# Query tiles of a hybrid decoder step taken from the last to the first

## Chip, cores and metric

The kernel runs on one core of a Trainium2 chip. The metric is the time of one execution in device microseconds. Before the change the median of three runs is 656.16 us (655.71 to 656.98).

## What is computed

One inference step of a one-layer decoder for a prompt of 1024 tokens and 8 samples of one new token each, model width 1024, all in float32. Cut to what matters:

```python
h = rmsnorm(x); q, ckv, skv, wkv, gate_logits, za, u, zp = split(h @ w_in)
# (A) 8 query heads, 2 key heads, head size 64; per head and query block of 128
k_c, v_c = compress_blocks(ckv)                       # 63 compressed blocks of the prompt
o_c = softmax(q k_c, causal) v_c
o_s = softmax(q skv_k, causal, top 16 blocks of 64) skv_v   # 16 blocks: all of the prompt
o_w = softmax(q wkv_k, causal, last 512) wkv_v
o_attn = g0 * o_c + g1 * o_s + g2 * o_w               # g = sigmoid(gate_logits)
# (B) pooling over trailing windows of 2, 4, 8, 16 tokens
o_pool = ((window_mean(u) - u) @ w_pool) * pool_scale
mix = concat(o_attn * silu(za), o_pool * silu(zp))
y = rmsnorm(x + mix @ w_out)
```

The new keys, values and pooling states are outputs too.

## The kernel before

Every product is made of high and low parts of its factors, so it costs three products on TensorE (two where one operand holds both parts). The work runs in stages: norm, transposes and token-major projections of x; compressed keys and values; queries, which go out to scratch memory; the eight samples ("decode"); the pooling group with its gate; and, from 292.6 us on, attention over the prompt. Only this last stage is touched by the change.

**Units.** Attention runs over `UNITS` (line 686): for each query tile i of 128 tokens, i from 0 to 7, four pairs of heads j. Tile i sees i+1 selected blocks of 128 keys, the last five at most as window blocks, and 64 compressed keys. So tile 0 has 2 blocks a unit and tile 7 has 13.

**stage1** (line 702) makes the scores S of a unit (line 736; groups of at most 512 columns, through three PSUM banks), masks them and takes their maxima on VectorE (line 699), exponentiates on ScalarE (line 750) and scales by sum and gate on GpSimd (line 756), which gives the tiles Ps (compressed and selected) and Pw (window). **stage2** (line 829) transposes the result block by block (lines 845, 853), splits it into high and low part on ScalarE and VectorE (lines 847 to 859: pc, ph, pl), multiplies by the values (lines 864 to 871) into bank O, and at the end adds the two halves of O (lines 875 to 883) and multiplies by the gate, if that is there already. stage1 of the next unit runs inside stage2 of the present one.

**The filler** (`filler`, line 1039) is a generator of steps of three products on TensorE that stand between those of attention. First `za_fill` (line 916): the gate path, 12 chunks (a quarter of the gate's columns by a chunk of tokens, in the order of `ZORD`) of 8 steps each, over tokens 0 to 383, 384 to 767 and 768 to 1031 (`CHUNKS`); each chunk ends in `gate` (a tanh on ScalarE, line 902, and products on VectorE and GpSimd, lines 910 and 912). Once a chunk of x has been used by all four quarters, `load_wo` (line 936) puts rows of the output weights in its place, those that `WROWS` lists, and splits them (lines 947 and 948). Then `out_half` (line 1022): the output product of a tile, by halves of 512 columns, eight steps each; rows 4 to 7 of the weights' row blocks (the pooling part) first, then rows 0 to 3 (attention's part). `split_m` (line 959) splits the mixed output on ScalarE and GpSimd, `out_add` and `out_end` add x, norm and store. Tile 0 and the samples (tile 8) come first, then tiles 1 to 6, each only after its attention is done (`done`); of tile 7 the pooling part is made ahead, and its attention part closes the kernel (line 1134 on). All filling products share one PSUM bank, pj.

**What sets the order.** The program is planned by a scheduler that estimates times; attention has priority, filling steps get in where it would wait, and `paced_fill` (line 1081) gives out steps at a rate per unit: 0.8 times (blocks + 2) in the gate path, 0.5 times (blocks + 2) in the output products, 12 at the start. Each engine then works through its own list strictly in order. Query tiles (`load_q`) are loaded on SP's queue four units ahead.

Of the kernel before, what the change touches and what calls it, by code (L numbers as in the profile page):

```python
# [20 lines left out]
D = 1024  # L21
NEG = -1.0e9
# pacing of the filling products: steps per block of attention (gate path, output), blocks added per unit,
# steps at the start, lag in products
NZ, NO, C0, OW, PLAG = 0.8, 0.5, 2, 12, 100
ZORD = ([(0, 0), (0, 1), (0, 2), (1, 0), (1, 1), (1, 2)]
        + [(pt, c) for c in range(3) for pt in (2, 3)])
# the rows of the output weights, by half of their columns, that take the place of each chunk of x
WROWS = [[(0, k) for k in (4, 5, 6, 7, 0, 1)], [(0, 2), (0, 3)] + [(1, k) for k in (4, 5, 6, 7)],
         [(1, k) for k in range(4)]]  # L30
C_Q, C_C, C_S, C_W, C_G, C_ZA, C_U, C_ZP = 0, 512, 768, 1024, 1280, 1304, 1816, 2328
# [10 lines left out]
def hybrid_step_kernel(ctx, tc, xp, xs, ccmp, cslc, cwin, spool, ptab, norm_g, w_in, cmp_pe, cmp_w1,  # L42
# [33 lines left out]

    # DRAM scratch
    q_d = dram.tile([2, 512, T], F32, name="q_d")
# [3 lines left out]

    # constants
    ident = pers.tile([128, 128], F32, name="ident")
# [7 lines left out]
    def ptr_rms(pool, ssq, n, name):  # L92
        """(ssq / D + eps) ** -0.5 for a [n, 1] column."""
        st = pool.tile([128, 2], F32, name=name, tag="rms", bufs=4)
        nc.gpsimd.tensor_scalar(st[:n, 0:1], ssq, 1.0 / D, 1e-6, op0=OP.mult, op1=OP.add)
        nc.gpsimd.tensor_tensor(st[:n, 1:2], st[:n, 0:1], mhalf[:n], op=OP.pow)
        return st[:n, 1:2]

    # persistent data
    KT = pers.tile([128, 2, KLEN], F32R, name="KT")  # L100
# [64 lines left out]
    def spread_g(h):  # L165
        """The norm's weights from the first partition to all."""
        cs = slice(h * 512, h * 512 + 512)
        p = ps_any()
        nc.tensor.matmul(p, ones, gb[0:1, cs], start=True, stop=True)
        if h:  # L170
            nc.scalar.activation(gb[:, cs], p, AF.Copy)
        else:
            nc.vector.tensor_copy(gb[:, cs], p)

    # masks
    nc.gpsimd.memset(mslc, 0.0)
# [10 lines left out]

    # normalised x, transposed, as high and low parts
    rss = {}
# [35 lines left out]

    # token-major projections: compressed, selected and window keys and values, gate logits
    def tok_unit(hi, lo, cn, t, mid=None):
# [112 lines left out]
    nc.gpsimd.dma_start(g_d[:, :], gates[:NB, 8, :])  # L340
    # a token before the end of the first compressed block has no compressed branch
    vgate = pers.tile([128, 24], F32, name="vgate")
# [27 lines left out]
    def silu2(out, src):  # L370
        """2 * silu(src)"""
        nc.scalar.activation(out, src, AF.Tanh, scale=0.5)
        nc.vector.scalar_tensor_tensor(out, out, 1.0, src, op0=OP.add, op1=OP.mult)

    # page indices: row of 2 tokens each
    pti = keep.tile([128, NB], I32, name="pti")
# [10 lines left out]

    # compressed keys and values, prompt and samples
    ces = ExitStack()
# [98 lines left out]

    # queries
    for pt in range(4):  # L490
# [18 lines left out]
    def decode():  # L509
        """One new token per sample."""  # L510
        dp = des.enter_context(tc.tile_pool(name="dp", bufs=1, reuse_waits="tile"))
        # queries, one column per head and sample; qx: high parts, then low parts, per sample
        qs = dp.tile([128, NB, 8], F32, name="qs")
# [6 lines left out]
        def diag(ap):  # L520
            """The columns of each sample's own heads in [b, 2, 64] columns: [p, b, h]."""
            return bass.AP(tensor=ap.tensor, offset=ap.offset, ap=[ap.ap[0], [136, NB], [1, 8]])
# [59 lines left out]
        for br in range(2):  # L582
# [6 lines left out]
            for b in range(0, NB, 2):  # L589
# [8 lines left out]
                for bb in range(2):  # L598
# [7 lines left out]
                    for par in range(2):  # L606
                        nc.tensor.transpose(p[:, (bb * 2 + par) * 128:(bb * 2 + par + 1) * 128],
                                            f[:, par * 256:par * 256 + 128], ident)
                    # high and low parts of the values
                    v = dp.tile([128, 2, 2, 128], F32R, name="vx", bufs=8)  # L610
# [72 lines left out]

    # pooling group
    at = ctx.enter_context(tc.tile_pool(name="at", bufs=2, reuse_waits="tile"))
    UNITS = [(i, j) for i in range(8) for j in range(4)]
    q_tiles = {}
# [14 lines left out]
    def stage1(i, pr_):  # L702
        """Scores and softmax of a pair of heads for 128 queries; yields between matmul groups."""
        kv = pr_ // 2
# [6 lines left out]
        sm = at.tile([128, 2, 4, 3], F32, name="sm", bufs=3)  # L711
        # the first tile of a head: compressed 0:64, selected 64:64+n; the second: window 0:wn
        c_m = mc[:, 56 - 8 * i:120 - 8 * i]
# [47 lines left out]
    for g in range(4):  # L761
# [31 lines left out]
        if g == 2:  # L793
            load_q(0, 0)
            load_q(0, 1)
        if g == 3:
# [9 lines left out]
        for c in range(3):  # L806
# [7 lines left out]
            else:  # L814
                # the last on the engine that stores them
                nc.scalar.activation(bb[:, cs], p[:, :n], AF.Copy, scale=psc[:, g:g + 1])
# [5 lines left out]

    # attention over the prompt; the gate path, the new tokens and the output projection fill in
    zap = ctx.enter_context(tc.tile_pool(name="zap", bufs=1, reuse_waits="tile"))
# [4 lines left out]
    def stage2(i, pr_):  # L829
        """Transposes, products with the values and their sum; a list of steps."""  # L830
        kv = pr_ // 2
# [63 lines left out]

    # tiles of za that hold one factor of the gated output: the gate or the attention's output
    half_done = set()
# [38 lines left out]
    def load_wo(c):  # L936
        """Output weights in the place of x's chunk c, which is no longer needed."""
        rows = WROWS[c]
# [20 lines left out]
    def split_m(i, part):  # L959
        """High and low parts of four of the eight row blocks of the mixed output."""  # L960
        op = O_["p"]
# [77 lines left out]
    def filler():  # L1039
        yield from za_fill()  # L1040
        open_out()
        first = 0
        st = {}, {}
        for half in range(2):
            yield from out_half(first, half, st[0])
            yield from out_half(8, half, st[1])
        for i in range(1, 7):
            while done.get(i, 99) > now[0]:
                yield None
            st = {}  # L1050
            for half in range(2):
                yield from out_half(i, half, st)
        # the last tile: the pooling part ahead of its attention
        tail["r"] = load_r(7)
        m = parts(7, 1)
        tail["p"] = ps_j(), ps_s("pj2")
# [19 lines left out]
    def after(a, b):  # L1076
        """Keeps a behind b in their engine's order."""
        tc.add_manual_dep(a, b.name, mybir.DependencyInfo(
            mybir.DependencyClass.NoSync, mybir.DependencyReason.DATA), reason="order")

    def paced_fill(k):
        """Steps of the filler, none ahead of the attention's products emitted so far."""
        ins = nc.cur_bb.bb.instructions
# [49 lines left out]
    now[0] = 999  # L1133
    run(fill, 1000)
    L = 7
    op = O_["p"]
# [68 lines left out]
```

## Time and profile before

| | |
|---|---|
| Median of the runs | 656.16 us |
| Span of the profiled execution | 654.4 us |
| TensorE busy (PE) | 627.6 us, 96% |
| Weight loads busy (PEld) | 581.6 us, 89% |
| VectorE busy (DVE) | 426.0 us, 65% |
| ScalarE busy (ACT) | 361.0 us, 55% |
| GpSimd busy (POOL) | 266.8 us, 41% |
| Data moved | 65.1 MB, 100 GB/s in the mean |

The engines work side by side, so the shares are each of the whole span. PE and PEld are the products and the loads of their stationary operands, which overlap. A product's record lasts longer than the distance from its start to the next one's, since products are pipelined; the distance from start to start tells what one costs.

### The profile page before, as it was taken

Reading aid. Unit: us, or ns where it says so; the run is one execution under the profiler, and the core shown is the slowest. Engines: PE = TensorE matmul, PEld = TensorE weight load, DVE = VectorE, ACT = ScalarE, POOL = GpSimd, SP = SyncE. Lnnn points to the kernel's source line nnn. Section 1 sums busy time; section 2 is a strip of 40 time slices with the busy share of each in tenths; the row PEclk is TensorE's granted clock in tenths of the full one; section 3 lists DMA queues with packets and bytes.
Section 4 is the critical chain, followed back from the end, with each engine's and each line's share of the span. In section 5 each row is a group of like instructions: output and inputs, shape, how many; then the busy total and the mean of one; then the engine's idle time right before and its main releaser. Section 6 shows DMA issues by size and latency. Waiting matters only on the chain. (4 is left out here: it accounts for less than half of the span.)

```text
span 654.4 us, 12214 instructions
## 1 busy us (share of the span) xinstructions
PE 627.6 (96%) x4141; PEld 581.6 (89%) x4141; DVE 426.0 (65%) x1306; ACT 361.0 (55%) x930; POOL 266.8 (41%) x410
## 2 busy tenths in 40 slices
PE   6995999999999999999999899999999999999995
PEld 4995999999999999998999888788899999988984
DVE  5741234555526547575797998779888788877652
ACT  5652233444413234325788787767587677665641
POOL 5153001431207424104565666736454445454511
PEclk9997999999999999999999999999999999999999
DMA  8432302984524342243313437212022030101001
GB/s 274 147 100 56 102 16 76 310 274 118 162 72 135 84 142 70 94 132 98 97 33 98 130 113 238 86 34 82 32 83 97 18 97 18 65 17 66 18 34 64
DMA packets 65677, 65.14 MB, mean 100 GB/s; under 512 B 6423, under 2 KB 56927, under 8 KB 65575
## 3 DMA queue, kind: packets, MB, share of 16 engines
q1 hardware_dynamic: 55599, 44.53, 22.8%
q0 software_dynamic: 3968, 12.76, 6.0%
q10 hardware_dynamic: 6048, 7.08, 3.0%
q8 instruction: 33, 0.54, 0.3%
q14 instruction: 29, 0.24, 0.1%
HBM read 50.99 MB, written 15.68 MB: 102 GB/s over the span
## 5 line engine op out<-in xcount | busy, mean ns | idle before, releaser
L756 POOL TENSOR_SCALAR Ps<-Ps,sm,gates 128x64 f32<-128x64 f32 (+1 forms) x120 | 75.3, 639 | 111.1 <-DVE sm L752 77.3
L736 PE MATMUL S<-KT,qt 128*128 128x320 f32 (+10 forms) x400 | 98.3, 347 | 1.9 <-DVE sm L699 1.8
L859 DVE TENSOR_TENSOR pl<-tp,ph 128x512 fp32r<-128x512 f32 (+1 forms) x136 | 89.9, 670 | 13.5 <-ACT ph L858 12.4
L858 ACT ACTIVATE ph<-tp 128x512 fp32r<-128x512 f32 (+1 forms) x136 | 76.6, 579 | 35.2 <-PE tp L853 28.2
L365 PE MATMUL pa<-x,ws_hi 128*128 128x384 f32 (+1 forms) x288 | 93.6, 325 | 0.0
L366 PE MATMUL pa<-x,ws_hi 128*128 128x384 f32 (+1 forms) x288 | 92.8, 322 | 0.0
L367 PE MATMUL pa<-x,ws_lo 128*128 128x384 f32 (+1 forms) x288 | 92.6, 322 | 0.0
L750 ACT ACTIVATE Ps<-Ps,sm 128x64 f32<-128x64 f32 (+8 forms) x128 | 70.6, 554 | 28.2 <-DVE sm L748 26.7
L995 PE MATMUL pj<-wo,mh 128*128 128x512 f32 x256 | 82.6, 400 | 0.0
L871 PE MATMUL O<-pl,V 128*128 128x256 f32 x264 | 77.7, 311 | 1.0 <-DVE pl L859 0.9
L870 PE MATMUL O<-ph,V 128*128 128x256 f32 x264 | 74.2, 295 | 0.0
L736 PEld LDWEIGHTS S<-KT,qt 128*128 128x128 f32 x400 | 63.9, 189 | 8.8 <-DVE sm L699 2.8
L244 PE MATMUL pa<-w_hi,x 128*128 128x256 f32 (+1 forms) x192 | 57.7, 301 | 0.2 <-DVE V L317 0.2
L246 PE MATMUL pa<-w_hi,x 128*128 128x256 f32 (+1 forms) x192 | 56.9, 296 | 0.4 <-DVE x L217 0.4
L245 PE MATMUL pa<-w_lo,x 128*128 128x256 f32 (+1 forms) x192 | 56.1, 293 | 0.0
L366 PEld LDWEIGHTS pa<-x,ws_hi 128*128 128x128 f32 x288 | 54.2, 188 | 0.4 <-issue 0.2
L365 PEld LDWEIGHTS pa<-x,ws_hi 128*128 128x128 f32 x288 | 54.2, 188 | 0.3 <-DVE us L776 0.2
L367 PEld LDWEIGHTS pa<-x,ws_lo 128*128 128x128 f32 x288 | 54.1, 188 | 0.3
L871 PEld LDWEIGHTS O<-pl,V 128*128 128x128 f32 x264 | 49.7, 188 | 4.8 <-DVE pl L859 3.0
L870 PEld LDWEIGHTS O<-ph,V 128*128 128x128 f32 x264 | 49.9, 189 | 2.0 <-ACT ph L858 0.2
L995 PEld LDWEIGHTS pj<-wo,mh 128*128 128x128 f32 x256 | 45.1, 188 | 7.0 <-PE S L736 0.4
L995 PE MATMUL pj<-wo,ml 128*128 128x512 f32 x128 | 50.6, 395 | 0.1
(279 smaller groups left out, 1530.9 us busy)
## 6 DMA issues: line engine op xcount, KB each, us to landing
ws_raw<-in_w_in SPq DMA_DIRECT2D x32, 256.0 KB
qt<-q_d SPq DMA_DIRECT2D x64, 128.0 KB
x_t<-in_x_prompt SPq DMA_DIRECT2D x8, 512.0 KB
wo_raw<-in_w_out SPq DMA_DIRECT2D x8, 512.0 KB
r<-in_x_prompt SPq DMA_DIRECT2D x8, 512.0 KB
out<-r SPq DMA_DIRECT2D x7, 512.0 KB
q_d<-qhl ACTq DMA_DIRECT2D x8, 384.0 KB
out<-kvf ACTq DMA_DIRECT2D x5, 512.0 KB
```

What stands on the lines that cost most here:

```text
L244: nc.tensor.matmul(p[:n, :cn], xh[c][:, k, ts_], hi[:, k, :cn], start=k == 0, stop=False)
L365: nc.tensor.matmul(p[:, :n], hi[:, k, :], xh[c][:, k, :], start=k == 0, stop=False)
L366: nc.tensor.matmul(p[:, :n], hi[:, k, :], xl[c][:, k, :], start=False, stop=False)
L367: nc.tensor.matmul(p[:, :n], lo[:, k, :], xh[c][:, k, :], start=False, stop=k == 7)
L736: nc.tensor.matmul(S[:, :ln], qt[:, f, h, :], KT[:, kv, k0 + a:k0 + a + ln], start=f == 0, stop=f == 1)
L750: nc.scalar.activation(regs[br], regs[br], AF.Exp, bias=sm[:, hh, 1, br:br + 1], accum_out=sm[:, hh, 2, br:br + 1])
L756: nc.gpsimd.tensor_scalar(regs[br], regs[br], sm[:, hh, 3, br:br + 1], gsrc[:, k:k + 1], op0=OP.mult, op1=OP.mult)
L858: nc.scalar.activation(ph[:, :m], tp[:, :m], AF.Copy)
L859: nc.vector.tensor_sub(pl[:, :m], tp[:, :m], r32(ph[:, :m]))
L870: nc.tensor.matmul(O[:, :256], vv, ph[:, a * 256:(a + 1) * 256], start=False, stop=False)
L871: nc.tensor.matmul(O[:, :256], vv, pl[:, a * 256:(a + 1) * 256], start=False, stop=last)
L995: nc.tensor.matmul(p, a[:, k % 4, :], w, start=first and kk == 0, stop=last and kk == 2)
```

## The change

The query tiles are taken from 7 down to 0 (`UNITS`). What hangs on the order is mirrored: the first query loads are those of tile 7; the gate path takes the last chunk of tokens first (`ZORD`); the output weights come in an order that fits the chunks' new order of release (`WROWS`); the filler's first output tile is 7, for which it waits until its attention is done, then 6 down to 1; tile 0 closes the kernel. The pacing constants stay. Comments were removed, which changes nothing.

```diff
-ZORD = ([(0, 0), (0, 1), (0, 2), (1, 0), (1, 1), (1, 2)]
-        + [(pt, c) for c in range(3) for pt in (2, 3)])
-WROWS = [[(0, k) for k in (4, 5, 6, 7, 0, 1)], [(0, 2), (0, 3)] + [(1, k) for k in (4, 5, 6, 7)],
-         [(1, k) for k in range(4)]]
+ZORD = ([(0, 2), (0, 1), (0, 0), (1, 2), (1, 1), (1, 0)]
+        + [(pt, c) for c in (2, 1, 0) for pt in (2, 3)])
+WROWS = [[(1, k) for k in (6, 7, 0, 1, 2, 3)], [(0, k) for k in range(4)] + [(1, 4), (1, 5)],
+         [(0, k) for k in (4, 5, 6, 7)]]
...
-    UNITS = [(i, j) for i in range(8) for j in range(4)]
+    UNITS = [(i, j) for i in range(7, -1, -1) for j in range(4)]
...
-            load_q(0, 0)
-            load_q(0, 1)
+            load_q(7, 0)
+            load_q(7, 1)
...
-        first = 0
+        first = 7
+        while done.get(first, 99) > now[0]:
+            yield None
...
-        for i in range(1, 7):
+        for i in range(6, 0, -1):
...
-        tail["r"] = load_r(7)
-        m = parts(7, 1)
+        tail["r"] = load_r(0)
+        m = parts(0, 1)
...
-    run(fill, 1000)
-    L = 7
+    run(fill, 2000)
+    L = 0
```

The order of the instructions shows it in three places. Names: pj is the filling products' bank, x_88 to x_90 are the three chunks of x, ws_hi and ws_lo the gate's weights, S the scores, tp the transposes' bank, O attention's result, wo the output weights, mh and ml the parts of the mixed output.

TensorE where attention starts, before the change: after a first chunk of the gate path come the scores of the first units of tile 0.

```order
L927 MATMUL pj<-x_88,ws_lo 128x384
L736 MATMUL S<-KT,qt 128x192
L736 MATMUL S<-KT,qt 128x128
L736 MATMUL S<-KT,qt 128x192 x2
L736 MATMUL S<-KT,qt 128x128
L736 MATMUL S<-KT,qt 128x192
L736 MATMUL S<-KT,qt 128x128 x2
L736 MATMUL S<-KT,qt 128x192 x2
```

The same place after the change:

```order
L927 MATMUL pj<-x_90,ws_lo 128x264
L736 MATMUL S<-KT,qt 128x512 x2
L736 MATMUL S<-KT,qt 128x352
L736 MATMUL S<-KT,qt 128x512 x2
L736 MATMUL S<-KT,qt 128x352 x3
L736 MATMUL S<-KT,qt 128x512 x4
L736 MATMUL S<-KT,qt 128x352 x4
L925 MATMUL pj<-x_89,ws_hi 128x384
```

The scores in front are now those of tile 7, and the filling chunk ahead of them has 264 columns in place of 384.

TensorE in the small tiles, before: the products with the values of tile 0's last unit, scores of tile 1, and the filling burst that follows.

```order
L736 MATMUL S<-KT,qt 128x256 x2
L853 MATMUL tp<-ident,Pw 128x128
L864 MATMUL O<-pc,Vc 128x256
L870 MATMUL O<-ph,V 128x256
L871 MATMUL O<-pl,V 128x256
L870 MATMUL O<-ph,V 128x256
L871 MATMUL O<-pl,V 128x256
L736 MATMUL S<-KT,qt 128x320 x2
L736 MATMUL S<-KT,qt 128x256 x2
L736 MATMUL S<-KT,qt 128x320 x2
L845 MATMUL tp<-ident,Ps 64x128
L925 MATMUL pj<-x_88,ws_hi 128x384
```

After, in the first unit of tile 1, with scores of tiles 1 and 0, between two bursts of tile 2's output products:

```order
L736 MATMUL S<-KT,qt 128x320 x2
L853 MATMUL tp<-ident,Ps 128x128 x3
L871 MATMUL O<-pl,V 128x256
L870 MATMUL O<-ph,V 128x256
L871 MATMUL O<-pl,V 128x256
L853 MATMUL tp<-ident,Pw 128x128 x4
L736 MATMUL S<-KT,qt 128x256 x2
L736 MATMUL S<-KT,qt 128x192 x2
L845 MATMUL tp<-ident,Ps 64x128
L736 MATMUL S<-KT,qt 128x128 x2
L736 MATMUL S<-KT,qt 128x192 x2
L995 MATMUL pj<-wo_4559,mh_7579 128x512 x2
```

Rows of this kind have moved from the stage's beginning to its end, and what fills there are output products (line 995) in place of gate products (lines 925 to 927).

GpSimd where output weights are split (line 948), before, in tile 2, whose selected part has 384 columns:

```order
L948 TENSOR_TENSOR wo_4496<-wo_raw,wo_4496 128x512
L883 TENSOR_TENSOR za<-za,ou 128x128
L948 TENSOR_TENSOR wo_4496<-wo_raw,wo_4496 128x512 x2
L756 TENSOR_SCALAR Ps<-Ps,sm,gates 128x64
L756 TENSOR_SCALAR Ps<-Ps,sm,gates 128x384
L756 TENSOR_SCALAR Pw<-Pw,sm,gates 128x384
```

After, in tile 6, whose selected part has 896:

```order
L948 TENSOR_TENSOR wo_4559<-wo_raw,wo_4559 128x512
L883 TENSOR_TENSOR za<-za,ou 128x128
L756 TENSOR_SCALAR Ps<-Ps,sm,gates 128x64
L756 TENSOR_SCALAR Ps<-Ps,sm,gates 128x896
L756 TENSOR_SCALAR Pw<-Pw,sm,gates 128x640
L948 TENSOR_TENSOR wo_4559<-wo_raw,wo_4559 128x512 x2
```

The splits have moved from the small tiles' softmax into the large tiles'.

## Rows read from the trace of the kernel before

**Rows 1.** Busy time by stretch, four stretches of attention: us from start, length, engines, clock.

```profile
core 0: us, PE busy (x) PEld busy (x) DVE busy (x) ACT busy (x) POOL busy (x), PEclk, DMA share, GB/s
292.60:429.20 136.60, 131.47 (x880) 119.37 (x879) 108.80 (x459) 103.64 (x323) 80.48 (x138) 1.00 0.36 109
429.20:638.00 208.80, 208.78 (x1345) 188.22 (x1344) 166.91 (x513) 141.53 (x347) 100.11 (x143) 1.00 0.16 52
328.20:351.40 23.20, 23.05 (x159) 20.88 (x158) 20.43 (x89) 19.66 (x64) 13.09 (x26) 1.00 0.16 41
351.40:429.20 77.80, 74.34 (x497) 66.07 (x496) 64.59 (x235) 60.73 (x168) 50.12 (x75) 1.00 0.43 135
```

**Rows 2.** TensorE in order of time: start, duration, line, operation, count; wait in brackets.

```profile
298.16 2.08 PE L736 MATMUL S<-KT,qt 128*128 128x128 f32 x12 [0.41 <-DVE sm L699]
...
301.59 0.34 PE L925 MATMUL pj<-x,ws_hi 128*128 128x384 f32 x1
...
301.94 0.33 PE L927 MATMUL pj<-x,ws_lo 128*128 128x384 f32 x1
...
307.64 0.28 PE L925 MATMUL pj<-x,ws_hi 128*128 128x264 f32 x1
...
307.88 0.29 PE L927 MATMUL pj<-x,ws_lo 128*128 128x264 f32 x1
...
640.10 0.62 PE L995 MATMUL pj<-wo,mh 128*128 128x512 f32 x2
...
640.78 0.39 PE L995 MATMUL pj<-wo,mh 128*128 128x512 f32 x1
```

**Rows 3.** Engines in order of time around the weights' splits in tile 2.

```profile
365.33 3.00 POOL L948 TENSOR_TENSOR wo<-wo_raw,wo 128x512 fp32r<-128x512 f32 x2
365.48 1.72 DVE L948 TENSOR_TENSOR wo<-wo_raw,wo 128x512 fp32r<-128x512 f32 x1
...
369.61 0.39 PE L871 MATMUL O<-pl,V 128*128 128x256 f32 x1 [0.68 <-DVE pl L859]
...
371.93 0.41 PE L925 MATMUL pj<-x,ws_hi 128*128 128x384 f32 x1 [0.82 <-DVE za L910]
```

**Rows 4.** Groups by line and form, ScalarE and VectorE, from 290 us: total and mean.

```profile
L947 ACT ACTIVATE wo<-wo_raw 128x512 fp32r<-128x512 f32 x16 | 9.1, 622 | 1.6 <-DMA wo_raw<-in_w_out 1.6
L1009 ACT ACTIVATE junk<-r 128x512 bf16<-128x512 f32 x14 | 8.7, 622 | 1.1 <-DVE r L1007 1.1
L977 ACT ACTIVATE mh<-mb 128x512 fp32r<-128x512 f32 x8 | 5.0, 625 | 4.8 <-PE pj L995 4.8
L977 ACT ACTIVATE mh<-za 128x512 fp32r<-128x512 f32 x7 | 4.4, 629 | 0.1
L902 ACT ACTIVATE zt<-pj 128x384 f32<-128x384 f32 x8 | 3.9, 484 | 6.1 <-PE pj L927 6.1
L902 ACT ACTIVATE zt<-pj 128x264 f32<-128x264 f32 x4 | 1.6, 388 | 0.0
L1007 DVE TENSOR_TENSOR r<-r,pj 128x512 f32<-128x512 f32 x14 | 9.5, 680 | 1.7 <-PE pj L995 1.6
L1015 DVE SCALAR_TENSOR_TENSOR r<-r,rms,fg 128x1024 f32<-128x1024 f32 x7 | 9.5, 1354 | 3.2 <-POOL rms L96 3.2
L948 DVE TENSOR_TENSOR wo<-wo_raw,wo 128x512 fp32r<-128x512 f32 x8 | 8.3, 1032 | 0.1
L910 DVE SCALAR_TENSOR_TENSOR za<-zt,pj 128x128 f32<-128x128 f32 x27 | 6.5, 280 | 0.2 <-ACT zt L902 0.2
L910 DVE SCALAR_TENSOR_TENSOR zt<-zt,pj 128x128 f32<-128x128 f32 x5 | 1.2, 282 | 0.5 <-ACT zt L902 0.5
```

**Rows 5.** Busy time by stretch, as rows 1: the first unit of tile 1.

```profile
328.20:332.40 4.20, 4.05 (x30) 3.47 (x29) 4.09 (x18) 3.63 (x11) 1.39 (x3) 1.00 0.01 4
```

**Rows 6.** Busy time by stretch, as rows 1: two early stretches.

```profile
54.50:61.40 6.90, 0.07 (x1) 0.00 (x0) 0.17 (x1) 0.83 (x3) 1.57 (x3) 0.71 0.29 77
61.40:65.40 4.00, 3.70 (x16) 3.41 (x17) 1.61 (x4) 1.94 (x6) 2.03 (x2) 0.50 0.34 76
```

## Prediction

> **What bounds the kernel now.** I read the page's busy shares first, then the stretches by stage, then the waits of the small tiles. TensorE is busy for 627.6 of 654.4 us. The change leaves the first 292.6 us alone: up to the last product of the pooling stage the order on every engine is the one of before. What it reorders is the attention stage, 292.6 to 638.0 us, which falls into two halves [rows 1]. In the half of the small query tiles, 0 to 3 (292.60 to 429.20, 136.60 us), TensorE shows 131.47 us busy, so 5.13 us of open waiting. In the half of the large tiles, 4 to 7 (208.80 us), it shows 208.78. VectorE is loaded alike in both (0.797 and 0.799); ScalarE is not (0.759 against 0.678), nor GpSimd (0.589 against 0.479).
>
> A busy TensorE hides more than those 5 us, so I price attention by its key blocks. A unit (a query tile and a pair of heads) of tile i has i+1 selected blocks and at most 5 window blocks: 80 blocks in the 16 units of the small half, 184 in the large. I take the filling products out first. Their pitch, start to start, is 0.175 us at 384 columns, 0.12 at 264 and 0.227 at 512 [rows 2]. The gate path is 192 and 96 products of the first two kinds, 33.6 + 11.5 = 45.1 us, all in the small half; of the 416 output products 36 stand there by program order, 344 in the large half and 36 behind it, 8.2 and 78.1 us in the two halves. So attention costs 136.6 - 45.1 - 8.2 = 83.3 us for 80 blocks (1.04 us each) in the small half, and 208.8 - 78.1 = 130.7 us for 184 (0.71 each) in the large. Short score products explain part of the difference, waiting the rest.
>
> **The change part by part.** No product is added or removed: the instructions counted by kind are the same, but for three gate pieces, and the attention outputs that meet them, which change places as first and second factor. TensorE's own work is unchanged, and the end moves only by what it waits.
>
> *Large tiles first.* They now meet the gate path, 45.1 us, and by program order 188 output products, 42.7 us. At the 0.71 us that a block costs beside output products, attention is 130.7 us again: together 218.5 us.
>
> *The first unit.* Its scores and the next unit's were short products that waited 0.41 us on VectorE [rows 2]; now they are products of 512 and 352 columns, through the same three score banks, each emptied by VectorE. Where the emptyings are the slower side, TensorE waits in its own order. I bound the extra wait from 0 (the emptying runs on under the 21 filling products behind the scores) to 3 us (0.41 for each of the eight banks of a unit) and take 0.8, nearer the row's single wait.
>
> *The output weights' conversion.* The 16 splits of the output weights move from tiles 2 and 3 to tiles 7 and 6. Where they run now, VectorE's first one took 1.72 us beside two of GpSimd's that took 3.00 together; right behind, a product with the values waited 0.68 us on VectorE and a gate product 0.82 [rows 3]. Tiles 2 and 3 hold 3.46 of the 5.13 us of open waiting [rows 1], which I put down to this for the most part. In the large tiles there is more TensorE work per softmax to hide it, but GpSimd now has three of the splits, 4.5 us at the same 1.5 each, in one block with two splits of the mixed output. From 0 (all hidden) to 3 us (as now); I take 1.2, since the large tiles show 0.02 us of waiting [rows 1]. The early half: 218.5 + 2.0 = 220.5 us.
>
> *Small tiles last.* The rest of the output products, 192, fill here: 43.6 us where 53.3 us stood. The fills that left were the heavier ones for the other engines: gate and output weights cost ScalarE 3.9 + 1.6 + 9.1 = 14.6 us and VectorE 6.5 + 1.2 + 8.3 = 16.0, and the four splits of the last two gate tiles, of the size of an output weight's split on ScalarE (0.57) and of an output's addition on VectorE (0.68), 2.3 and 2.7 more: 16.9 and 18.7. All 416 output products cost ScalarE 5.0 + 4.4 + 8.7 = 18.1 and VectorE 9.5 + 9.5 = 19.0 [rows 4], of which 36/416 (1.6 us) were here and 192/416 (8.4 and 8.8) will be. VectorE's load goes from 108.8 to 108.8 - 18.7 - 1.6 + 8.8 = 97.3 us, ScalarE's from 103.6 to 103.6 - 16.9 - 1.6 + 8.4 = 93.5. If each keeps its present share of the half (0.797, 0.759), VectorE asks for 122.1 us and ScalarE for 123.2. The bounds: at the 0.88 that VectorE reaches over tile 1 (20.43 of 23.20) [rows 1] it would be 110 us; at attention's present 83.3 us it would be 126.9. I take 122.6, nearer the second, because over tiles 0 to 3 as a whole no engine holds tile 1's share.
>
> *Units without fill.* The filler may only touch tiles whose attention is done, and from tile 4 on it stands right behind it. By program order five units now have two filling products or fewer (the first and last of tile 3, the first of tile 2, the first two of tile 1); four units have three or fewer now. Such a unit runs at the pace of VectorE and ScalarE: the first of tile 1 takes 4.20 us, 4.09 of them busy on VectorE, 3.63 on ScalarE and 3.47 on the weight loads [rows 5]. One such unit more, at the 0.7 us by which it outlasts its weight loads, adds 0.7.
>
> *Queues.* The output weights' loads on SP's queue now stand ahead of the query loads of tile 5 rather than of tile 4, but query tiles are asked for four units ahead, some 50 us there and 16 to 20 us in the small tiles: nothing. GpSimd's results in the small tiles are hidden now by filling bursts of 24 products (4.2 us); in the new order by bursts of 12 (2.7 us). That is in the range.
>
> *The end.* Behind the last product of attention 37 output products stand now, 36 then, with the same chain of row sums and stores: -0.2 us.
>
> The sum: 220.5 + 122.6 + 0.7 - 0.2 = 343.6 us where 208.8 + 136.6 = 345.4 stood: -1.8 us, a span of 652.6 us. The profiled span is 654.4 us, the median of the runs 656.16: 1.8 us lie outside the span, so I forecast **654.4 us**.
>
> One rule speaks to how much is to be had. The large half is 100% busy by its matmuls, but its weight loads are busy for 0.901 of it, and 0.874 of the small half [rows 1]. The Trainium skill (Perfetto Trace Analysis, Identifying the Most-Contended Engine) says that matmul busy time is a bad measure of headroom and weight-load busy time a good one. By the trace the two say different things here, 5.1 us of waiting against a possible 136.6 - 119.37/0.901 = 4.1 us to bring the small half to the large one's density; by either, what shows openly is worth some 4 to 5 us, and a gain beyond it would have to come out of waiting that neither share shows.
>
> **The rivals.** *Slower: the holes.* The filler catches up with attention, so small units run bare, and the products it could have used have been spent on large tiles that showed no waiting. For it: tiles 0 and 1 now lean on 24-product bursts, and the tiles' last units get 0 to 2 products. Against it: 36 output products and the last tile's pooling half are left over as cover. Price: attention in the late half stays at 83.3 us (126.9 us) and the early extra is 4: 218.5 + 4 + 126.9 + 0.7 - 0.2 = 349.9, +4.5 us, 660.7 us. It decides from where the small tiles' attention costs more than 81 us.
>
> *No change.* What the conversion gains under the large tiles is lost again in the late half, at 124.4 us: 218.5 + 2.0 + 124.4 + 0.5 = 345.4, 656.2 us.
>
> *Much faster.* The late half runs at VectorE's 0.88 in part, 116 us: 218.5 + 2.0 + 116 + 0.5 = 337.0, -8.4 us, 647.8 us. For it: VectorE loses 11.5 us of work there and ScalarE 10.1. Against: tiles 2 and 3 held 64.59 of 77.80 us, 0.83, with longer units than tiles 0 and 1.
>
> *The clock.* One long wait, 6.90 us from 54.50 to 61.40, is followed by a granted clock of 0.50, the lower level, for 4.00 us [rows 6]; no wait in attention passes 1 us, and the clock there is 1.00. The Trainium skill (TensorE: Matmul & The Clock Gate, HAM oscillation — how this bites in real kernels) warns that repeated idle gaps between matmul bursts bring the lower level back; no wait that I expect in the late half is of that size. Were the clock at 0.50 for 8 us of the late half, it would cost 4 us: about 658.4 us.
>
> That the change does not do what it says is excluded by the order of the instructions.
>
> **How the numbers follow.** A measurement of this kernel can tell about 0.2%, 1.3 us. Forecast (1.3 to 7 us faster) 0.40; much faster 0.10; no change 0.22; the holes 0.26; the clock 0.02. So faster 0.50, same 0.22, slower 0.28. The range reaches from 648.5, inside the much faster case, to 660.7, the price of the holes; a tenth or less lies beyond either end.
>
> **What would show it.** Right: attention's stage at some 343.6 us; open TensorE waiting of 1 to 3 us in the first four tiles and below 4 in the last four; VectorE's share about 0.8 in both halves; the clock at 1.00. Wrong: open waiting over 6 us in the last 120 us of attention, on the softmax of bare units or on the splits of the mixed output (the holes); waits of a microsecond or more at the weights' conversion in tile 6; or a late half under 117 us. What would upset the sum most is attention per block beside gate products in the large tiles that isn't the 0.71 us it costs beside output products: 0.03 us a block is 5 us.

## The result

The changed kernel takes 660.15 us (median of six runs, 658.66 to 661.40) where the kernel before takes 656.02 beside it: a ratio of 1.0057, interval 1.0042 to 1.0072. I had forecast 654.4 us, 1.8 us faster; it is 4.1 us slower. That lies in the range and near the 660.7 us of the rival "the holes", but, as the trace shows, not for the reason that this rival gives.

The profiled spans are 654.4 and 659.3 us. Busy time by stretch after the change, cut as [rows 1] are, at the end of the half's last unit: first the four large tiles and the four small ones, then tile 7 and tile 6 alone. Columns: us from start, length, busy time and instructions of each engine, granted clock, DMA.

```profile
core 0: us, PE busy (x) PEld busy (x) DVE busy (x) ACT busy (x) POOL busy (x), PEclk, DMA share, GB/s
293.95:532.45 238.50, 234.92 (x1562) 215.07 (x1561) 191.37 (x640) 162.66 (x398) 111.50 (x154) 1.00 0.26 81
532.45:643.25 110.80, 107.25 (x664) 92.57 (x663) 86.60 (x332) 83.70 (x271) 67.89 (x126) 1.00 0.18 58
293.95:375.30 81.35, 80.10 (x543) 74.68 (x542) 62.13 (x218) 50.11 (x117) 31.37 (x41) 1.00 0.17 50
375.30:431.50 56.20, 54.22 (x363) 50.03 (x361) 45.63 (x147) 42.06 (x100) 32.73 (x40) 1.00 0.38 114
```

Attention takes 238.50 + 110.80 = 349.3 us where 345.4 stood [rows 1]. The large half, now first, shows 238.50 - 234.92 = 3.58 us of open waiting where it had 0.02; the small half 3.55 where it had 5.13. The clock is 1.00 throughout. Behind attention stand 16.1 us as against 16.4. The rest of the 4.9 us is that attention begins at 293.95 and not at 292.6; the order of the work ahead of it is the same, and in the 20 profiles of this study it begins anywhere from 292.1 to 294.8 us, so I count that as scatter.

TensorE's open waits during attention, after the change: who waits, for what, us in total, times, longest.

```profile
PE S L736 <- DVE sm L699: 3.4, 7, 0.9
PE tp L845 <- POOL Ps L756: 1.5, 2, 1.4
PE O L864 <- DVE ou L880: 0.8, 2, 0.4
PE pj L925 <- DVE sm L752: 0.6, 1, 0.6
```

Open waits are only a small part. For the rest I took each product's distance from its start to the next one's, less the distance that products of the same step and columns keep when nothing is late (their pitch: the 20th percentile in the kernels before and after), and summed what is over by tile. This is the **waiting** of the expectations below, in us:

| tile | 0 | 1 | 2 | 3 | 4 | 5 | 6 | 7 | 0 to 3 | 4 to 7 | sum |
|---|---|---|---|---|---|---|---|---|---|---|---|
| before | 6.9 | 5.2 | 7.6 | 11.7 | 8.6 | 8.4 | 9.3 | 9.3 | 31.4 | 35.5 | 66.9 |
| after | 3.8 | 5.2 | 8.8 | 7.8 | 7.8 | 9.2 | 13.3 | 14.6 | 25.6 | 44.9 | 70.5 |

The sum rises by 3.6 us, nearly the whole loss of the stage (3.9). The late half, where the rival saw it, waits 5.8 us less. The early half waits 9.4 more, all of it in tiles 7 and 6. By unit: the first of tile 7 waits 5.2 us where a late unit of it waited 2.4; the next three 9.4 where the last three waited 6.9; tile 6's first three 3.2, 3.6 and 4.0 us. The first is the start of the pipeline, the next three have gate products, the last gate products and the splits of the output weights. My theory was so: what makes TensorE wait went along into the large tiles and costs more there. The rival: holes, small units run bare. The runs tell more than either.

### The profile page after: what moved, and what is told of

It reads as the page before. It is cut to its first block, busy times and chain, and to the rows that moved or that the text cites. A ratio compares the mean times of both kernels' runs of the same rounds, so it can differ in the third digit from the quotient of the medians.

```text
span 659.3 us, 12195 instructions
## 1 busy us (share of the span) xinstructions
PE 631.0 (96%) x4141; PEld 583.1 (88%) x4141; DVE 428.4 (65%) x1306; ACT 362.4 (55%) x930; POOL 265.3 (40%) x410
```

## The weights' splits and the gate, taken out

Without the splits (both orders; `q_d` is the queries' scratch memory):

```diff
-            raw = rp.tile([128, 2, 512], F32, name="wo_raw", tag="r")
-            nc.sync.dma_start(raw, w_out[k * 128:(k + 2) * 128, half * 512:half * 512 + 512]
-                              .rearrange("(k p) c -> p k c", p=128))
+            for f in range(2):
+                nc.sync.dma_start(r32(w[:, f, j:j + 2]),
+                                  q_d[f, (k % 4) // 2 * 256:(k % 4) // 2 * 256 + 256, half * 512:half * 512 + 512]
+                                  .rearrange("(k p) c -> p k c", p=128))
...
-                nc.scalar.activation(w[:, 0, j + kk], raw[:, kk], AF.Copy)
-                (nc.vector, nc.gpsimd)[kk].tensor_sub(w[:, 1, j + kk], raw[:, kk], r32(w[:, 0, j + kk]))
```

> Changed kernel without the 16 splits of the output weights: in their place two loads of the same size bring ready numbers (queries from scratch memory instead of weights, so the output rows are not the reference's). ScalarE loses 9.1 us, VectorE 8.3 us, GpSimd the other eight splits. Theory (what makes TensorE wait went along into the large tiles and costs more there): tile 6 waits 13.3 us beyond its products' own pitch where it waited 9.3 us as a late tile; without the splits it comes down by 2.5 to 4 us, the time to about 656 to 657.5 us. Rival (the holes: bare units in the late half): tile 6 may gain, but no more than the kernel before gains in the same way, so the distance of about 4 us between the two orders stays.

> Kernel before with the same part left out (ready numbers loaded in place of the output weights and their 16 splits). Theory: the splits cost TensorE less beside small tiles; tiles 2 and 3 wait 19.3 us now and 16.5 us as late tiles, so at most 1 to 2.5 us are gained: 653.5 to 655 us. Rival: it gains as much as the changed kernel does, 3 us or more: 653 us or less.

The times went the other way, with less work: 661.67 us (ratio 1.0095, 1.0074 to 1.0116), 1.5 us above the changed kernel's 660.15, and 662.07 (1.0096, 1.0075 to 1.0116), 6.1 above the unedited runs beside it. The three units beside the splits did what the theory said. Busy time over units 4 to 6, with the splits (the changed kernel) and, in the second fence, without:

```profile
375.30:417.84 42.54, 40.62 (x276) 37.78 (x275) 34.05 (x114) 32.84 (x77) 25.03 (x31) 1.00 0.36 108
```

```profile
373.70:411.93 38.23, 38.23 (x273) 37.59 (x272) 30.77 (x107) 26.63 (x62) 17.04 (x25) 1.00 0.43 132
```

Nearly the same number of products takes 4.3 us less, and the open waiting of 1.92 us is gone; by pitch the three units wait 6.8 us in place of 10.8, 2.3 each, as every large unit does. So the splits cost the changed kernel 3.9 us. Tile 6 as a whole comes down by only 1.9, since its last unit now waits 4.6 us in place of 2.6. In the kernel before, units 8 to 14 wait 12.9 in place of 17.2: 4.3 us. They cost as much in either order, which is the rival's claim, not mine. What was won came back elsewhere, for the order of the later instructions is planned anew. In the changed kernel it is that last unit of tile 6 and the late half, which waits 2.9 us more, with an open wait of 2.83 us for a split of the mixed output on GpSimd (shown at the end). In the kernel before a split of the mixed output now stands on ScalarE for a load, with TensorE behind it (start, duration, engine, line, operation; in brackets the wait and what ended it):

```profile
416.64 0.63 ACT L976 ACTIVATE mh<-mb 128x512 fp32r<-128x512 f32 x1 [5.66 <-DMA mb<-b_d]
417.33 1.22 PE L994 MATMUL pj<-wo,mh 128*128 128x512 f32 x2 [5.67 <-ACT mh L976]
```

The doubled loads of these two kernels may have held that load up; that isn't shown, and a wait of the same kind stands further down in a kernel without them. Without the gate's work on VectorE and GpSimd:

```diff
-        nc.scalar.activation(zt[:, :n], p[:, :n], AF.Tanh, scale=0.5)
...
+        for a0, a1, to_z in spans:
+            nc.scalar.activation(zt[:, a0:a1] if to_z else za[:, pt, t0 + a0:t0 + a1], p[:, a0:a1],
+                                 AF.Tanh, scale=0.5)
...
-            nc.vector.scalar_tensor_tensor(z if both else a, z, 1.0, p[:, c:c + m], op0=OP.add, op1=OP.mult)
-            if both:
-                nc.gpsimd.tensor_mul(a, z, as_t[:, pt, :] if i == 8 else a)
```

> Changed kernel without the gate's work on VectorE and GpSimd (32 products of VectorE, 7.7 us, and GpSimd's products): the tanh on ScalarE writes the gate directly, so the outputs are not the reference's; TensorE's work stays. Theory: units 1 to 3 of tile 7 wait 9.4 us where they waited 6.9 us as last units; that and part of tile 6 comes back, 2 to 3.5 us: 656.5 to 658 us. Rival (the holes): under 1 us, 659 us or more, since the late half is untouched.

> Kernel before with the same part of the gate left out. Theory: beside the small tiles the gate's products cost TensorE little: 0 to 1.5 us gained, 654.5 to 656 us. Rival: as much as in the changed kernel.

The changed kernel takes 669.31 us (1.0224, 1.0193 to 1.0255), the kernel before 655.51 (0.9996, 0.9980 to 1.0012). Units 1 to 3 of tile 7 come down from 9.4 to 7.4 us, which is the 2 us of the theory; but the first unit now waits 10.4 us, since ScalarE splits gate weights (L139) ahead of attention's high part and TensorE stands 2.14 us for it, after which the granted clock falls. The sum goes to 78.2 us. By the time, the run says nothing on the gate; by its three units, the gate's products cost some 2 us there.

## The order of the tiles alone

The first two edits change the tiles' order; the first loads, the filler's order of tiles and the closing tile follow it (the dots stand for that), while the gate path and the weights' places stay as in the changed kernel and in the kernel before. The third leaves the changed order and puts those two back.

```diff
-    UNITS = [(i, j) for i in range(7, -1, -1) for j in range(4)]
+    UNITS = [(i, j) for i in (4, 5, 6, 7, 0, 1, 2, 3) for j in range(4)]
...
```

> Changed kernel with the tiles in the order 4, 5, 6, 7, 0, 1, 2, 3: the large half still comes first, but nothing is mirrored within the halves; tile 3 closes the kernel. Theory (what counts is that the start, the gate path and the weights' splits stand beside large tiles): as slow as the changed kernel or slower, 658.5 to 662 us, TensorE waiting 43 us or more beyond its products' pitch in the first four tiles. Rival (the loss comes from the mirrored end, small bare units behind a filler that has caught up): tiles 2 and 3 with their longer units stand last, the loss goes, 656.5 us or less.

```diff
-    UNITS = [(i, j) for i in range(8) for j in range(4)]
+    UNITS = [(i, j) for i in (3, 2, 1, 0, 7, 6, 5, 4) for j in range(4)]
...
```

> Kernel before with the tiles in the order 3, 2, 1, 0, 7, 6, 5, 4: the small half first, as before, but mirrored within the halves; tile 4 closes the kernel. Theory: near the kernel before, 654 to 658 us, with about 31 us of waiting in the first four tiles and 35 in the last four. Rival (mirroring itself costs): 659 us or more.

```diff
-ZORD = ([(0, 2), (0, 1), (0, 0), (1, 2), (1, 1), (1, 0)]
-        + [(pt, c) for c in (2, 1, 0) for pt in (2, 3)])
+ZORD = ([(0, 0), (0, 1), (0, 2), (1, 0), (1, 1), (1, 2)]
+        + [(pt, c) for c in range(3) for pt in (2, 3)])
...
+WROWS = [[(0, k) for k in (4, 5, 6, 7, 0, 1)], [(0, 2), (0, 3)] + [(1, k) for k in (4, 5, 6, 7)],
+         [(1, k) for k in range(4)]]
```

> Changed kernel with the gate path's chunks and the output weights' places as in the kernel before, so that the tiles' order alone is changed. Theory: it makes no difference which chunk of tokens the gate path takes beside tile 7, 659 to 661.5 us. Rival (the mirrored chunks, which meet the attention's outputs of tiles 6 and 7 the other way round, cause the loss): 657 us or less.

The first takes 664.61 us (1.0131, 1.0112 to 1.0150) with 45.5 us of waiting in the four large tiles in front and 25.5 in the small ones, the same as the changed kernel's 44.9 and 25.6: the large half in front waits so much without the tiles being mirrored inside the halves. (Of the 4.5 us by which it is slower still, 2.1 are a wait for a split of the mixed output at the very end.) The second takes 674.75 us (1.0289, 1.0271 to 1.0307) and goes against the theory: the small half in front waits 41.2 us, not 31, and the large one 41.5. The third takes 669.94 us (1.0219, 1.0183 to 1.0256) where both sides expected 661.5 or less: the mirrored gate path isn't the cause; without it the changed order takes 9.8 us more. In these last two kernels the granted clock also falls during attention, to 0.50: in the second twice, for 3.4 and 10.2 us, in the third three times, for 3.4 us each. Six of these seven edits had now come out slower than the kernel they were made in, most of them in ways that neither theory names.

## Splits on GpSimd, the holes, the start

```diff
-                (nc.vector, nc.gpsimd)[kk].tensor_sub(w[:, 1, j + kk], raw[:, kk], r32(w[:, 0, j + kk]))
+                nc.gpsimd.tensor_sub(w[:, 1, j + kk], raw[:, kk], r32(w[:, 0, j + kk]))
```

> Changed kernel with all 16 splits of the output weights on GpSimd, where eight of them stand on VectorE now. Units 4 to 6, beside which they stand, wait 3.2, 3.6 and 4.0 us and without any split 2.3 each. Theory (the wait comes by way of VectorE, whose splits of 1.0 us stand ahead of the score reductions and of the low parts): 2 us or more come back in these units, 656.5 to 658.5 us. Rival (GpSimd, which scales the softmax and takes 1.3 us for a split, is then the late one): no gain or a loss in these units, 660 us or more.

> Kernel before with all 16 splits of the output weights on GpSimd. Units 8 to 14 wait 17.2 us and without any split 12.9. Theory (by way of VectorE): about 2 us come back there, 653.5 to 655 us, which would be faster than both kernels. Rival (GpSimd becomes the late one): 656 us or more.

669.65 us (1.0180, 1.0155 to 1.0205) and 663.39 (1.0092, 1.0073 to 1.0111): by the time, the rival's side. By unit the theory has something too: in the changed order units 4 and 5 wait 2.5 and 2.8 us in place of 3.2 and 3.6, but unit 6 4.4 in place of 4.0 and unit 7 7.6 in place of 2.6. The late half also waits 6 us more, and the clock falls three times in attention, of which only the first stands behind unit 7's wait. That wait shows a mechanism that I had not thought of. VectorE and GpSimd side by side, first in the changed order, then in the order before; L748 negates three numbers per partition, L978 is GpSimd's split of the mixed output.

```profile
415.87 5.05 POOL L948 TENSOR_TENSOR wo<-wo_raw,wo 128x512 fp32r<-128x512 f32 x4
...
417.52 0.42 DVE L848 TENSOR_TENSOR pc<-tp,pc 64x256 fp32r<-64x256 f32 x1
...
418.57 3.60 DVE L748 TENSOR_SCALAR sm<-sm 128x3 f32<-128x3 f32 x1
...
420.86 1.28 POOL L978 TENSOR_TENSOR ml<-mb,mh 128x512 fp32r<-128x512 f32 x1
...
422.96 0.41 PE L853 MATMUL tp<-ident,Ps 128*128 128x128 f32 x2 [3.39 <-DVE pl L859]
```

```profile
365.07 5.17 DVE L748 TENSOR_SCALAR sm<-sm 128x3 f32<-128x3 f32 x1
365.19 5.02 POOL L948 TENSOR_TENSOR wo<-wo_raw,wo 128x512 fp32r<-128x512 f32 x4
...
370.95 0.58 PE L871 MATMUL O<-pl,V 128*128 128x256 f32 x1 [2.89 <-DVE pl L859]
```

In the second the small instruction lasts 5.17 us and ends with the last of GpSimd's four splits (370.24 and 370.21); in the first it lasts 3.60 us, through the rest of two splits of the weights and the one of the mixed output behind them. All 64 of its kind, in the kernels before and after the change, first the one before (duration min/median/max in ns):

```profile
L748 DVE TENSOR_SCALAR sm<-sm x64: 127/168/580, 298.5 to 613.5; 128x3 f32<-128x3 f32 x64
```

```profile
L748 DVE TENSOR_SCALAR sm<-sm x64: 153/169/1243, 301.4 to 628.5; 128x3 f32<-128x3 f32 x64
```

Where this instruction begins inside one of GpSimd's splits, it mostly ends with the split, 0.02 to 0.03 us behind it, and everything on VectorE's queue stands. In the changed kernel that happens to seven of the eight that begin so, 0.34 to 1.24 us each, in the kernel before to one of five with more than 0.2 us (0.45): by 0.17 us for an undisturbed one, 4.2 us of VectorE's time against 0.3; with GpSimd's other instructions, beside which the same is seen, it is 6.2 against 2.6 over all 64. How much of the 3.6 us comes by this way wasn't tried by itself. With twice the weights' splits on GpSimd it gets worse, and the expected 2 us are not to be had so.

```diff
-NZ, NO, C0, OW, PLAG = 0.8, 0.5, 2, 12, 100
+NZ, NO, C0, OW, PLAG = 0.8, 0.4, 2, 12, 100
```

> Changed kernel with the output products given out at 0.4 steps per block in place of 0.5: some 38 of the 188 that stand beside the large tiles move to the small ones, TensorE's work is the same. Theory: the late half has little left to gain, 659 to 661 us. Rival (the holes: small units run bare because their cover was spent on the large tiles): bare units are filled, 657.5 us or less.

658.52 us (1.0037, 1.0024 to 1.0049), 1.6 us under the changed kernel. The first 431 us are unchanged; the late half waits 22.7 us in place of 25.6, and tiles 5 and 4 give back 1.5. So the holes are there, and filled they are worth 2.9 us in their place and 1.6 net: too much for the theory, which had 659 us or more, too little for the rival.

```diff
-NZ, NO, C0, OW, PLAG = 0.8, 0.5, 2, 12, 100
+NZ, NO, C0, OW, PLAG = 0.8, 0.5, 2, 24, 100
```

> Changed kernel with 24 steps of the gate path given out at the start in place of 12, so that 36 more products (6.3 us) stand beside the first units of tile 7. The first unit waits 5.2 us, 2.9 more than a unit of tile 7 waits as a late one. Theory (the first scores wait on their way through the score banks, and filling products cover that): the first unit comes down to 4 us or less, the time to about 659 us. Rival (the wait is the softmax of a large unit with nothing attention can do in the meantime but short of cover nowhere): no change in the first unit, 660 us or more.

661.12 us (1.0063, 1.0048 to 1.0077). The first four units didn't change at all, filling product by filling product: as I read the code, the lag behind attention (PLAG), not what is owed, sets what they get. This doesn't test the start. But from unit 4 on the plan differs: units 4 to 6 wait 7.7 us in place of 10.8, units 7 and 15 to 17 wait longer, and the sum ends at 71.8.

The two edits of a_no40 and a_convpool in one:

> Changed kernel with both: 0.4 steps per block of output products and all splits of the output weights on GpSimd. If each gives what the theory has for it (1.6 us measured for the first, about 2 for the second), 656.5 us, level with the kernel before; if the splits on GpSimd cost as much as they save, 658.5 us.

662.17 us (1.0069, 1.0049 to 1.0088): 3.6 us above a_no40, so the splits on GpSimd cost here too: the same open wait, 3.4 us, and one fall of the clock behind it.

## The same edits in the kernel before

Nearly everything tried had made things slower, whichever order it was tried in. So the question turned: is the large tiles' order slow, or is the plan of the kernel before a good draw, or one that its constants were chosen for?

The kernel before got the two pacing edits above, and both orders a third one:

> Kernel before with 0.4 steps per block of output products in place of 0.5. The first 428 us of it keep their plan but for the last units of tile 3. Theory (the order itself costs): 655 to 657 us, some 2 us or more under the changed order with the same edit (658.5 us). Rival (the kernel before is a good draw): 658 us or more.

> Kernel before with 24 steps of the gate path at the start in place of 12. Theory (the order itself costs): 655 to 658 us, 3 us or more under the changed order with the same edit (661.1 us). Rival (a good draw, lost by any edit): 659 us or more.

```diff
-NZ, NO, C0, OW, PLAG = 0.8, 0.5, 2, 12, 100
+NZ, NO, C0, OW, PLAG = 0.7, 0.5, 2, 12, 100
```

> Kernel before with 0.7 steps per block in the gate path in place of 0.8, so that the weights' splits come a unit or so later. Theory (the order itself costs): 655 to 658 us, 2 us or more under the changed order with the same edit. Rival (a good draw): 659 us or more, level with the changed order.

> Changed kernel with 0.7 steps per block in the gate path in place of 0.8; part of the weights' splits come beside tile 5. Theory (the order itself costs): 659 to 662 us, since start, gate path and splits still stand beside large tiles. Rival (a draw): anything from 656 to 668 us, and level with the kernel before under the same edit.

Medians in us:

| edit | tiles 0 to 7 | tiles 7 to 0 | difference |
|---|---|---|---|
| none | 656.02 | 660.15 | +4.1 |
| output steps 0.4 | 662.29 | 658.52 | -3.8 |
| 24 steps at the start | 665.54 | 661.12 | -4.4 |
| gate steps 0.7 | 661.04 | 659.32 | -1.7 |
| splits on GpSimd | 663.39 | 669.65 | +6.3 |
| mean | 661.66 | 661.75 | +0.1 |

Two pairs are left out, since their kernels lack work: without the splits the difference is -0.4 us, without the gate's work +13.8. With them the mean of seven is +2.0, so the mean itself rests on which edits one takes.

The ratios to the unchanged kernel before are 1.0088 (1.0057 to 1.0120), 1.0138 (1.0100 to 1.0176) and 1.0068 (1.0043 to 1.0094) for the three pacing edits of it, and 1.0042 (1.0023 to 1.0060) for the changed order with 0.7.

The rival won, and my theory fell. A small change of pacing costs the kernel before 4.7 to 9.2 us against its unedited runs beside it; the changed order moves by -1.6 to +1.0 against its 660.15 under the same three. With each of them the changed order is the faster, though with 0.7 the two intervals overlap, and the changed order's 659.32 fits the theory's own range.

Two things blur this. The edits weigh unequally: with 0.4 about 60 products more stand behind attention in the order before, 36 in the changed one. And part of the losses is the clock: in the order before it falls during attention for 6.8 us with 24 steps and for 3.4 with 0.7, in the changed order for 3.4 with 0.7. The one fall of 3.4 us that is worked out at the end lost 1.6 us. With 0.4 it doesn't fall; there the order before waits 5.5 us more in attention, 2.7 of it in tile 4 and 1.7 in tile 7.

Where another such loss sits is shown by the order before with 24 steps at the start: a split of the mixed output on ScalarE (L972) gets in ahead of attention and waits for its load, VectorE and TensorE wait in turn, and the clock falls.

```profile
415.56 0.23 ACT L972 ACTIVATE m<-mb 128x32 fp32r<-128x32 f32 x1 [3.89 <-DMA mb<-b_d]
415.70 0.58 ACT L858 ACTIVATE ph<-tp 128x512 fp32r<-128x512 f32 x1
...
416.31 0.69 DVE L859 TENSOR_TENSOR pl<-tp,ph 128x512 fp32r<-128x512 f32 x1 [4.18 <-ACT ph L858]
...
417.05 1.11 PE L853 MATMUL tp<-ident,Pw 128*128 128x128 f32 x4 [3.64 <-DVE pl L859]
```

Two last kernels combine pacing edits in the changed order (0.7 and 0.4; 0.4 and 24):

> Changed kernel with 0.7 gate steps and 0.4 output steps per block. If the two edits add up: 660.15 - 0.8 - 1.6 = 657.7 us, within 1 us. If each combination is a plan of its own, the time lies anywhere from 655 to 663 us.

> Changed kernel with 0.4 output steps per block and 24 steps at the start. The latter takes the waits of units 4 to 6 from 10.8 to 7.7 us but gave them back later. If the edits add up: 660.15 - 1.6 + 1.0 = 659.5 us, within 1 us. If each combination is a plan of its own: anywhere from 655 to 663 us; at 656 us or less it would be level with the kernel before.

664.67 us (1.0124, 1.0109 to 1.0138), 7 us off the sum: a plan of its own. And 657.14 us (1.0009, 1.0001 to 1.0018), 2.4 under the sum and 0.1% above the kernel before, with 67.3 us of waiting where that one has 66.9. None of the variants with its full work beats the kernel before.

## Why the prediction was wrong

**What bounds the kernel.** That TensorE sets the time and that only its waiting moves was right: over all of attention its products, each at its undisturbed pitch, need the same 278 us in both kernels. But I said that open waiting, or the share of the weight loads, told some 4 to 5 us to be had. The Trainium skill (Perfetto Trace Analysis, Identifying the Most-Contended Engine) says to judge TensorE by weight-load busy time and the share of peak FLOPs, not by matmul busy time. I used the first only to compare the halves: 4.1 us of room in the small one, which did gain 5.8 when it moved to the end. But the large half was no mark to measure by: its weight loads leave 208.80 - 188.22 = 20.6 us of it free [rows 1], and by the distances 35.5 us of it are waiting, behind a busy share of 1.00.

**Large tiles first, 218.5 us.** The cost per block, 0.71 and 1.04 us, was taken between two cuts at unit ends, but scores are made a unit ahead: 228 score products stand in the large half of the kernel before [rows 1] and 286 in that of the changed one, some 9 us at their pitch. That put 9 us into the wrong half and cancels in the sum; with the early extra below it is most of why the halves came out at 238.50 in place of 220.5 us and 110.80 in place of 123.3 (122.6 + 0.7). It also hid what I had said would upset the sum most.

**The early extra, 2.0 us: the step that failed.** It measured 9.4 us. The first unit took 2.9 (I took 0.8, bounds 0 and 3). The weights' splits took 3.9 (I took 1.2, bounds 0 and 3): the bound came from open waits [rows 3], and half of what the splits cost doesn't show openly. Units 1 to 3 beside the gate took 2.5, which I had priced at nothing, though I had named it as what would upset the sum most. I took the 0.02 us of open waiting in the large tiles [rows 1] for cover, and it was none.

**The late half, -3.6 us.** It measured -5.8: tile 0 lost its start (-3.1), tile 3 the splits and the first output products (-3.9), and bare units cost tile 2 1.1 us. Nothing of the load argument by VectorE's and ScalarE's share was needed. So the start and the splits cost about the same in either place: 2.9 us early against 3.1 given back, 3.9 against 4.3 (the kernel before without splits). What is not given back, the 2.5 us beside the gate and tile 2's 1.1, is the stage's 3.6. This is arithmetic over two plans, not an experiment.

**The end, -0.2 us,** was right (16.4 and 16.1 us behind the last unit). **Queues:** right that no query load was late.

**The rivals.** "The holes" had the time and not the way: it put the early extra at 4 us and the late half at no gain. The clock stayed at 1.00 during attention in both kernels, as forecast; in the profiles of eleven of the eighteen experiments it didn't.

**What no step had.** The pacing constants and the plan were those of the old order, and under most of the edits tried the time moved by several microseconds. My range was worked out as if only the named terms moved; that the result still lies just inside it is luck. Settled is where the 4 us of this pair lie, by tile. That the order of the tiles costs anything by itself isn't shown: with four other edits that keep the full work it was faster three times, and the mean of the five pairs differs by 0.1 us. Nor is it shown that it costs nothing. Why the kernel before at just these constants is the best of its neighbours, by a lucky plan or by constants chosen for it, stays open, and the start of the pipeline with a large tile wasn't tested alone.

## What to carry over

In a program whose order a planner makes, a change that moves work must be priced against the spread of plans: give both sides the same two or three small neutral edits before a few microseconds are put down to the change. Waiting is to be read start to start, against the pitch of the same product when nothing is late; an engine that is 100% busy hid 35 us by this measure. And a bound read from open waits is no upper bound.

## What the runs showed of the chip that I had not expected

**A small VectorE instruction waits out GpSimd's splits, several in a row.** L748 on VectorE, from SBUF to SBUF, 0.17 us in the median, lasted 3.60 and 5.17 us while three and four splits of GpSimd ran one behind the other. Not every VectorE instruction does: L848, which reads PSUM, took 0.42 us beside the same splits. The Trainium skill (SBUF — State Buffer, SBUF: two separate sides) says that GpSimd shares a pair of ports with VectorE instructions that run in a two-port mode or have two inputs in SBUF, as an exclusive lock: the one that starts first holds it for its whole instruction and the other blocks fully. The blocking agrees, though no run here shows in which mode L748 ran; the trace adds that the blocked instruction didn't get in between GpSimd's instructions.

**A lower clock followed waits of some 3 us and less, and not always.** I had thought of waits of 7 us. Here an open wait of 2.82 us for GpSimd's split was followed by the lower level, in the changed order with the gate path as before (the wait, then stretches of 2 us):

```profile
636.62 0.50 PE L995 MATMUL pj<-wo,ml 128*128 128x512 f32 x1 [2.82 <-POOL ml L978]
```

```profile
634.00:636.00 2.00, 0.00 (x0) 0.00 (x0) 2.00 (x4) 0.62 (x3) 2.00 (x2) 1.00 0.03 14
636.00:638.00 2.00, 1.38 (x5) 1.15 (x6) 1.94 (x6) 1.21 (x6) 1.63 (x4) 0.89 0.61 248
638.00:640.00 2.00, 2.00 (x6) 1.51 (x6) 0.22 (x2) 1.21 (x6) 2.00 (x6) 0.50 0.00 0
640.00:642.00 2.00, 2.00 (x14) 1.86 (x13) 1.02 (x2) 0.71 (x3) 1.07 (x3) 0.76 0.00 0
```

The same place in the changed order without the splits, after an open wait of 2.83 us for the same split:

```profile
628.25 0.50 PE L994 MATMUL pj<-wo,ml 128*128 128x512 f32 x1 [2.83 <-POOL ml L977]
```

```profile
625.00:627.00 2.00, 0.41 (x2) 0.11 (x1) 1.95 (x6) 1.24 (x4) 2.00 (x4) 1.00 0.00 0
627.00:629.00 2.00, 0.75 (x3) 0.66 (x4) 1.66 (x6) 1.47 (x8) 2.00 (x4) 1.00 0.63 262
629.00:631.00 2.00, 2.00 (x12) 1.68 (x12) 0.33 (x2) 0.95 (x6) 2.00 (x5) 1.00 0.02 4
```

The ten output products behind the wait and the start of the next took 3.67 us (636.62 to 640.29) and 2.40 us (628.25 to 630.65), 1.3 us more; to the start of the output product that comes next in both (641.76 and 631.80) it is 1.6 us for one fall. In the changed order with 0.7 gate steps it followed a wait of 1.61 us that ended at 428.52 (granted clock 0.86, 0.50 and 0.79 in the stretches of 2 us from 428); in the changed kernel none followed one of 1.37 us.
